# A hybrid decoder layer in float32: another order of the seven products of a block multiplication, with accumulation banks by name

## The chip, the cores and the metric

The kernel runs on one core of one Trainium2 chip. The metric is the device time in microseconds (us); the median of several runs counts. TensorE does the matrix products into PSUM, which has eight banks of 128 x 512 float32; ScalarE (ACT), VectorE (DVE) and GpSimd (POOL) do the element-wise work; nearly all transfers are issued on SyncE's queue (SP).

## The reference, cut to what matters

One layer of a decoder, for 1024 positions and a width of 2048:

```
mod = silu(c) @ W_ada + b_ada              -> shift, scale, gate
h   = rms_norm(x, gain) * (1 + scale) + shift
proj = h @ W_in                            # 2048 x 8192: q k v z (stick-breaking), q k v z (retention)
oa = stick_breaking_attention(norm(q), norm(k), v) * silu(z)    # 8 heads of 128
ob = group_norm(chunkwise_retention(rot(q), rot(k), v)) * silu(z)   # 8 heads of 128
out = x + gate * (concat(oa, ob) @ W_out)  # 2048 x 2048
```

All inputs and the output are float32.

## The kernel before

**Matrix products.** Both large projections are made by a two-by-two block scheme with seven products instead of eight (Winograd's form). The left side is h (or the concatenated heads), transposed, over half of the inner width (1024); its seven block combinations A11, S1, S2, S3, S4, A12, A22 stay in SBUF, each in four pieces of 128 x 512 and each piece as a rounded high part and a low part (`split`: ScalarE makes the high part, L123; VectorE or GpSimd the low part, L124). The right side is a block of 256 columns of the weights, called a *group*. `Group.right` forms what each product needs of it (T1 and T2 on GpSimd), `Group.product` splits it and issues 12 matmuls of 128 x 512 (`mm3`, L127 to L129: four pieces, three matmuls each). The high parts of the weights have four buffers (`wh`), the low parts three (`wl`).

Four results come out of each group, two column halves (i) by two row halves (hf). They are built up in three banks: b takes P1, then P6, then P5, then P3 on top of each other, d takes P7 and then P4, and a takes P2. Between the products the bank is read:

- after P1, ScalarE copies b (`copied`, L272) to p1, and after P2 VectorE adds bank a to it (`added`, L280, or L282 with a gate): result (0,0)
- after P6, ScalarE copies b to u2, and after P4 VectorE adds d: result (0,1)
- after P5, ScalarE copies b to u4 and VectorE adds d: result (1,1)
- after P3, b holds result (1,0), c12

A matmul that adds to a bank, or begins it anew, waits until the bank has been read. The banks are taken in turn from four buffers of one tag, `pj`; the other four banks (A0, A1, B, C) serve the attention work.

**Streams.** `stream` runs a list of groups. P3 and P4 of a group come after P1 of the next one, and after the last group they stand alone. There are five streams: e (16 groups, first half of the inner width, stick-breaking columns; results to `part`), then 32 groups in one stream (f: 16 groups, second half of the inner width, with e's results added to them as a seed, which completes the stick-breaking columns; g: 16 groups, second half, retention columns, results to `part`), then c (16 groups named f too in the profile: first half, whose left side was put by in `keep`, with g's results as a seed, which completes the retention columns; its q and k results are turned by rotary tables in `second_put`, L697 to L703, and written out at L704), then y and o (8 groups each, the two halves of the output projection). The seed is loaded by `old` (L264) and added by GpSimd (L274) behind the copy, or, for c12, by VectorE.

**What sets the order.** TensorE's instructions run in the order in which the program issues them. After each three matmuls of the stream, `run` calls `tick()`, which lets the tasks of two lanes issue their own work (attention heads, preparation of the conditioning, placing of the next left side). The order on the other engines and on SP's queue is chosen by the scheduler of the tile framework, by readiness and priority; products, copies and sums carry a high priority (AHEAD). At the end of a stream, `take` and `gather` replace each left combination as soon as its last product of the stream is issued (`tell`), and the list there gives that order. Tiles of one tag go round over a fixed number of buffers: `pt` (copies, 4 in the streams before the last), `cp` (seeds, 2).

**Retention.** `ret_heads` issues, for each head, the turning of k (`turn_k`), the state updates (`states`), scores (`scores_r`), values (`values_r`) and the normed output's transposes (`finish`), six ticks apart, in banks A0, A1, B and C.

Of the kernel before, what the change touches and what calls it, by code (L numbers as in the profile page):

```python
# [27 lines left out]
RSQRT_MAGIC = 1597463007.0  # L28
AHEAD = 4000
NP = 4  # L30
COMBOS = ("A11", "S3", "S2", "A12", "S1", "S4", "A22")
LEFT = {"P1": "A11", "P7": "S3", "P6": "S2", "P2": "A12", "P5": "S1", "P3": "S4", "P4": "A22"}
SB_GAP = 8
RT_GAP = 6
# [9 lines left out]
def layer_kernel(ctx, tc, x, c, w_ada, b_ada, norm_gain, w_in, sb_q_gain, sb_k_gain, ret_norm_gain, w_out,  # L44
# [158 lines left out]
    class Group:  # L203
# [13 lines left out]
        def right(self, p):  # L217

            t = self.t
            if p == "P1":  # L220
                self.load(0)
                return t["B11"]
            if p == "P7":
                self.load(1)
                t["T1"] = t1 = wp.tile([P, NP, P], F32, tag="wt", bufs=3, name=f"t1_{self.name}")
                nc.gpsimd.tensor_tensor(t1, t["B12"], t["B11"], op=ALU.subtract)
                nc.gpsimd.tensor_tensor(t["B12"], t["B22"], t["B12"], op=ALU.subtract)
                return t["B12"]
            if p == "P6":
                t["T2"] = t2 = wp.tile([P, NP, P], F32, tag="wt", bufs=3, name=f"t2_{self.name}")  # L230
                nc.gpsimd.tensor_tensor(t2, t["B22"], t["T1"], op=ALU.subtract)
                return t2
            if p == "P2":
                return t["B21"]
            if p == "P5":
                return t["T1"]
            if p == "P3":
                return t["B22"]
            nc.gpsimd.tensor_tensor(t["T2"], t["B21"], t["T2"], op=ALU.subtract)
            return t["T2"]  # L240
# [13 lines left out]

    pp = None

    def bank(name):
        return ps.tile([P, HALF], F32, tag="pj", bufs=4, name=name)

    def old(g, i, hf):  # L260

# [2 lines left out]
        nc.sync.dma_start(t, g.seed[i][:, hf * HALF:(hf + 1) * HALF])  # L264
        return t

    def copied(g, src, i, hf, name):

        pool, bufs, _ = g.pool
        t = pool.tile([P, HALF], F32, tag="pt", bufs=bufs, name=f"{name}_{g.name}")  # L270
        gt = g.gate[i]
        nc.scalar.activation(t, src, AF.Copy, scale=1.0 if gt is None else gt)  # L272
# [10 lines left out]

    def stream(groups, after=None):

        prev = None
        tell = after or (lambda n: None)
        for g in list(groups) + [None]:
            if g is not None:
                last = g is groups[-1]  # L290
                if last:
                    tell("")
                g.b = bank(f"b_{g.name}")
                yield from g.product("P1", g.b, True)
                with tc.high_priority(AHEAD):
                    g.p1 = copied(g, g.b, 0, 0, "p1")
                if last:
                    tell("A11")
            if prev is not None:
                q = prev  # L300
                yield from q.product("P3", q.b, False)
                with tc.high_priority(AHEAD):
                    if q.seed is None:
                        c12 = copied(q, q.b, 1, 0, "c12")
                    else:
                        c12 = old(q, 1, 0)
                        added(q, c12, q.b, 1)
                    q.put(1, 0, c12)
                if g is None:
                    tell("S4")  # L310
                yield from q.product("P4", q.d, False)
                with tc.high_priority(AHEAD):
                    added(q, q.u2, q.d, 0)
                    q.put(0, 1, q.u2)
                if g is None:
                    tell("A22")
                if q.done:
                    q.done()
            if g is not None:
                g.d = bank(f"d_{g.name}")  # L320
                yield from g.product("P7", g.d, True)
                if last:
                    tell("S3")
                yield from g.product("P6", g.b, False)
                with tc.high_priority(AHEAD):
                    g.u2 = copied(g, g.b, 0, 1, "u2")
                if last:
                    tell("S2")
                a = bank(f"a_{g.name}")
                yield from g.product("P2", a, True)  # L330
                with tc.high_priority(AHEAD):
                    added(g, g.p1, a, 0)
                    g.put(0, 0, g.p1)
                if last:
                    tell("A12")
# [136 lines left out]
    def first_half(j):  # L472
        for e in range(2):
            for g in range(2):
                to_h(xT[2 * j + e, g], 2 * j + e)
        sums = combine(xT[2 * j, 0], xT[2 * j + 1, 0], xT[2 * j, 1], xT[2 * j + 1, 1],
                       lambda n: st.tile([P, HALF], F32, tag="ht", bufs=7, name=f"{n}_{j}"),
                       nc.vector if j == NP - 1 else nc.gpsimd)
        for n in ("A11", "S3", "S2", "A12", "S1", "A22", "S4"):
            place(n, j, sums[n])  # L480

    x_norms(0)
# [396 lines left out]
    def ret_heads():  # L879
# [5 lines left out]
        for h in range(NH):  # L885
# [33 lines left out]
                                                       up[:, j * P:(j + 1) * P], op0=ALU.mult, op1=ALU.add)  # L919

            def scores_r(g):
                sp = ps.tile([P, 4, P], F32, tag=f"A{g}", name=f"sp_{h}_{g}")
                for j in range(4):
                    tk = slice(j * P, (j + 1) * P)
                    nc.tensor.matmul(sp[:, j, :], k[g][:, tk], q[g][:, tk], start=True, stop=True)
                pTs[g] = pT = ht("T", f"pT{g}")
                nc.vector.tensor_tensor(pT, sp, dm.rearrange("p (a n) -> p a n", a=1).broadcast_to([P, 4, P]),
                                        op=ALU.mult)

            def values_r(g):  # L930
                pT = pTs.pop(g)
                op = ps.tile([P, 4, P], F32, tag=("B", "C")[g], name=f"op_{h}_{g}")
                for j in range(4):
                    cidx = 4 * g + j
                    nc.tensor.matmul(op[:, j, :], pT[:, j, :], v[:, cidx, :], start=True, stop=(cidx == 0))
# [16 lines left out]
                return on, loaded(halves(7 * NH + h, g), f"rz_{h}_{g}")  # L952

            def finish(h, g, on, z):
                tp = ps.tile([P, HALF], F32, tag=("A0", "B")[g], name=f"otp_{h}_{g}")
                for j in range(4):
                    nc.tensor.transpose(tp[:, j * P:(j + 1) * P], on[:, j, :], ident)
                nc.vector.scalar_tensor_tensor(z, tp, ret_g[:, h:h + 1], z, op0=ALU.mult, op1=ALU.mult)
# [53 lines left out]
    start(heads(), 1, 0)  # L1012

    def take(src, needs=()):
        order = ("A11", "S3", "S2", "A12", "S1", "S4", "A22")
        coming = {}

        def tell(n):

            while not needs <= ready:  # L1020
                tick()
            nxt = order[order.index(n) + 1] if n and n != order[-1] else None if n else order[0]
# [104 lines left out]
```

## Time and profile before

| | us |
|---|---|
| median of 3 runs | 2125.51 (2122.24 to 2126.42) |
| profiled execution, its own time | 2124.26 |
| its span, first to last instruction | 2122.3 |
| TensorE busy (matmuls, modelled ends) | 1948.8 (92%) |
| VectorE busy | 1415.7 (67%) |
| ScalarE busy | 965.0 (45%) |
| GpSimd busy | 961.0 (45%) |

A row of waits has the waiting engine, tile and line, then what ended the wait, then the total in us, how often, and the longest. Tile names have their numbers left out: `b_f` is bank b of a group f, `u_f` is u2 or u4, `S_h` the high part of S1 to S4. PE is TensorE, PEld its weight loads. A window's row has the stretch, its length, TensorE's busy time with its instructions, the granted share of its clock, the transfers' share and GB/s.

### The profile page before, as it was taken

To read this page: it belongs to the slowest core of one execution; us is meant where nothing else is said; L and a number is where in the kernel's file an instruction comes from. 1 tells how busy PE (TensorE), PEld (TensorE's weight loads), DVE (VectorE), ACT (ScalarE), POOL (GpSimd) and SP (SyncE) were. 2 spreads that over 40 slices of the span, in tenths; PEclk is the share of its full clock that TensorE was granted. 3 is DMA by queue.
4 is the path that set the end of the run, shared out by engine and by line. 5 is a ranking of instruction groups with operands and counts; after the bars stand their busy time and mean duration, and the time that the engine had idled before them with its cause. 6 is when DMAs were issued, how large, how long until landed. Compare 5 with 4: busy or idle time off the path is not lost. (4 is left out here: it accounts for less than half of the span.)

```text
span 2122.3 us, 28088 instructions
## 1 busy us (share of the span) xinstructions
PE 1948.8 (92%) x9025; PEld 1585.5 (75%) x9025; DVE 1415.7 (67%) x2221; ACT 965.0 (45%) x1771; POOL 961.0 (45%) x850
## 2 busy tenths in 40 slices
PE   5889899898999999999999997898989889998998
PEld 4467777777878777788878885686868767887887
DVE  6677866467768676766564658765776767557554
ACT  5444344354455646455454555453443445335322
POOL 1335575555544544432423244646454453234442
PEclk9879999998999999999999998899999999999999
DMA  9647877423555555563454366656766677556664
GB/s 308 209 159 255 258 256 229 136 86 123 183 156 164 165 164 164 166 192 118 161 160 138 115 206 191 203 168 221 222 221 225 220 235 246 169 173 202 220 208 145
DMA packets 293671, 400.02 MB, mean 188 GB/s; under 512 B 32810, under 2 KB 164980, under 8 KB 293524
## 3 DMA queue, kind: packets, MB, share of 16 engines
q1 hardware_dynamic: 293120, 398.19, 58.6%
q8 instruction: 71, 1.16, 0.2%
q14 instruction: 76, 0.62, 0.1%
q10 hardware_dynamic: 404, 0.05, 0.0%
HBM read 290.05 MB, written 108.10 MB: 188 GB/s over the span
## 5 line engine op out<-in xcount | busy, mean ns | idle before, releaser
L754 DVE TENSOR_TENSOR_SCAN om<-om 128x128 f32<-128x128 f32 (+2 forms) x96 | 107.2, 1117 | 99.6 <-POOL om L744 77.2
L127 PE MATMUL b_f<-S_h,wh_f_P 128*128 128x512 f32 x384 | 157.8, 411 | 15.5 <-ACT u_f L272 15.5
L129 PE MATMUL b_f<-S_h,wl_f_P 128*128 128x512 f32 x384 | 154.3, 402 | 3.9 <-DVE wl_f_P L124 3.9
L128 PE MATMUL b_f<-S_l,wh_f_P 128*128 128x512 f32 x384 | 154.1, 401 | 0.0
L274 POOL TENSOR_TENSOR u_f<-u_f,cp_f 128x512 f32<-128x512 f32 x64 | 88.6, 1385 | 110.5 <-ACT u_f L272 109.5
L124 DVE TENSOR_TENSOR wl_f_P<-wr_f,wh_f_P 128x512 fp32r<-128x512 f32 x128 | 115.6, 904 | 16.6 <-PE b_f L129 4.6
L380 DVE SCALAR_TENSOR_TENSOR acc_b<-ada_b,silu_c,acc_b 128x512 f32<-128x512 f32 x88 | 90.3, 1026 | 37.3 <-DMA ada_b<-in_w_ada_dram 35.7
L123 ACT ACTIVATE wh_f_P<-wr_f 128x512 fp32r<-128x512 f32 x128 | 80.4, 629 | 71.2 <-PE b_f L128 49.1
L127 PEld LDWEIGHTS b_f<-S_h,wh_f_P 128*128 128x128 f32 x384 | 74.6, 194 | 35.8 <-ACT u_f L272 21.2
L127 PE MATMUL b_e<-S_h,wh_e_P 128*128 128x512 f32 x192 | 79.0, 411 | 16.1 <-ACT u_e L272 12.4
L129 PEld LDWEIGHTS b_f<-S_h,wl_f_P 128*128 128x128 f32 x384 | 74.8, 195 | 21.6 <-DVE wl_f_P L124 5.0
L124 DVE TENSOR_TENSOR wl_f_P<-t_f,wh_f_P 128x512 fp32r<-128x512 f32 x96 | 80.7, 841 | 14.1 <-PE b_f L129 11.4
L127 PE MATMUL b_g<-S_h,wh_g_P 128*128 128x512 f32 x192 | 76.2, 397 | 11.2 <-ACT u_g L272 11.1
L128 PEld LDWEIGHTS b_f<-S_l,wh_f_P 128*128 128x128 f32 x384 | 74.7, 195 | 14.6
L123 ACT ACTIVATE wh_f_P<-t_f 128x512 fp32r<-128x512 f32 x96 | 60.2, 628 | 54.9 <-PE a_f L128 16.0
L758 DVE TENSOR_TENSOR be<-be,om 128x128 f32<-128x128 f32 (+2 forms) x96 | 69.5, 724 | 23.3 <-POOL be L746 18.2
L129 PE MATMUL b_e<-S_h,wl_e_P 128*128 128x512 f32 x192 | 78.4, 408 | 5.2 <-DVE wl_e_P L124 5.2
L123 ACT ACTIVATE wh_e_P<-wr_e 128x512 fp32r<-128x512 f32 x64 | 40.2, 628 | 89.9 <-PE b_e L128 65.8
L741 ACT ACTIVATE om<-zp,rq 128x128 f32<-128x128 f32 (+2 forms) x96 | 55.8, 582 | 52.2 <-PE zp L129 36.3
L798 PE MATMUL oT<-a,v 128*128 128x256 f32 x320 | 78.9, 386 | 0.0
L128 PE MATMUL b_e<-S_l,wh_e_P 128*128 128x512 f32 x192 | 77.6, 404 | 0.0
L129 PE MATMUL b_g<-S_h,wl_g_P 128*128 128x512 f32 x192 | 75.7, 394 | 0.1
(388 smaller groups left out, 6407.0 us busy)
## 6 DMA issues: line engine op xcount, KB each, us to landing
ada_b<-in_w_ada_dram SPq DMA_DIRECT2D x128, 256.0 KB
cp_f<-part SPq DMA_DIRECT2D x128, 256.0 KB
wr_f<-in_w_in_dram SPq DMA_DIRECT2D x64, 512.0 KB
wr_e<-in_w_in_dram SPq DMA_DIRECT2D x32, 512.0 KB
ada_a<-in_w_ada_dram SPq DMA_DIRECT2D x64, 256.0 KB
fin<-u_f SPq DMA_DIRECT2D x64, 256.0 KB
wr_g<-in_w_in_dram SPq DMA_DIRECT2D x32, 512.0 KB
vT<-fin SPq DMA_DIRECT2D x48, 256.0 KB
```

The lines of the kernel that those rows point to most:

```text
L123: nc.scalar.activation(hi, src, AF.Copy)
L124: eng.tensor_tensor(lo, src, hi.bitcast(F32), op=ALU.subtract)
L127: nc.tensor.matmul(o, a_hi, b_hi, start=first, stop=False, skip_group_check=True)
L128: nc.tensor.matmul(o, a_hi, b_lo, start=False, stop=False, skip_group_check=True)
L129: nc.tensor.matmul(o, a_lo, b_hi, start=False, stop=last, skip_group_check=True)
L274: nc.gpsimd.tensor_tensor(t, t, old(g, i, hf), op=ALU.add)
L380: nc.vector.scalar_tensor_tensor(acc, src, cj, acc, op0=ALU.mult, op1=ALU.add)
L741: nc.scalar.activation(om[:, :n], zp[:, :n], AF.Sigmoid, scale=rq[:, h, 1, i:i + 1])
L754: nc.vector.tensor_tensor_scan(rev, rev, rev, init, op0=ALU.mult, op1=ALU.bypass)
L758: nc.vector.tensor_tensor(be[:, :n], be[:, :n], om[:, 1:n + 1], op=ALU.mult)
L798: nc.tensor.matmul(ob, v[:, j, :], a[:, cl], start=diag and ib == 0 and b == 0 and j2 == 0, stop=ch == 0 and ib == 2, skip_group_check=True)
```

## The change

The order of the products in the stream is P1, (of the group before: P4, P3), P6, P7, P2, P5 instead of P1, (P3, P4), P7, P6, P2, P5. With it go the lists `COMBOS`, the order of placing in `first_half` and the list in `take`, which become one list `ORDER`.

The fourth result (1,1), u4, is begun by a copy of bank d after P7, and bank b is added to it after P5; before, it was begun by a copy of b after P5, and d was added.

The banks have names: b goes to pj1 and pj0 in turn, and d and a to pj3 and pj2, exchanged from group to group. The turning of x at the start (`turn_x`) takes pj0, A1, pj1, pj2, B, pj3 in turn.

T2 is formed right behind T1, for P6. The copy c12 of groups without a seed takes a `cp` buffer instead of a `pt` buffer.

In retention, `scores_r(0)` takes B instead of A0, `values_r(0)` A0 instead of B, and `finish` of the first half B instead of A0.

```diff
-COMBOS = ("A11", "S3", "S2", "A12", "S1", "S4", "A22")
+ORDER = COMBOS = ("A11", "S2", "S3", "A12", "S1", "A22", "S4")
...
-            if p == "P7":
+            if p == "P6":
                 self.load(1)
                 t["T1"] = t1 = wp.tile([P, NP, P], F32, tag="wt", bufs=3, name=f"t1_{self.name}")
                 nc.gpsimd.tensor_tensor(t1, t["B12"], t["B11"], op=ALU.subtract)
+                t["T2"] = t2 = wp.tile([P, NP, P], F32, tag="wt", bufs=3, name=f"t2_{self.name}")
+                nc.gpsimd.tensor_tensor(t2, t["B22"], t1, op=ALU.subtract)
+                return t2
+            if p == "P7":
                 nc.gpsimd.tensor_tensor(t["B12"], t["B22"], t["B12"], op=ALU.subtract)
                 return t["B12"]
-            if p == "P6":
-                t["T2"] = t2 = wp.tile([P, NP, P], F32, tag="wt", bufs=3, name=f"t2_{self.name}")
-                nc.gpsimd.tensor_tensor(t2, t["B22"], t["T1"], op=ALU.subtract)
-                return t2
...
-    def bank(name):
-        return ps.tile([P, HALF], F32, tag="pj", bufs=4, name=name)
+    def bank(i, name):
+        return ps.tile([P, HALF], F32, tag=f"pj{i}", name=name)
...
-                g.b = bank(f"b_{g.name}")
+                n += 1
+                g.b = bank(n % 2, f"b_{g.name}")
                 yield from g.product("P1", g.b, True)
...
+                yield from q.product("P4", q.d, False)
+                with tc.high_priority(AHEAD):
+                    added(q, q.u2, q.d, 0)
+                    q.put(0, 1, q.u2)
...
                 yield from q.product("P3", q.b, False)
                 with tc.high_priority(AHEAD):
                     if q.seed is None:
-                        c12 = copied(q, q.b, 1, 0, "c12")
+                        c12 = copied(q, q.b, 1, 0, "c12", "cp")
...
-                yield from q.product("P4", q.d, False)
-                with tc.high_priority(AHEAD):
-                    added(q, q.u2, q.d, 0)
-                    q.put(0, 1, q.u2)
...
-                g.d = bank(f"d_{g.name}")
-                yield from g.product("P7", g.d, True)
...
                 yield from g.product("P6", g.b, False)
                 with tc.high_priority(AHEAD):
                     g.u2 = copied(g, g.b, 0, 1, "u2")
...
-                a = bank(f"a_{g.name}")
+                g.d = bank(2 + n % 2, f"d_{g.name}")
+                yield from g.product("P7", g.d, True)
+                with tc.high_priority(AHEAD):
+                    u4 = copied(g, g.d, 1, 1, "u4")
...
+                a = bank(3 - n % 2, f"a_{g.name}")
                 yield from g.product("P2", a, True)
...
                 yield from g.product("P5", g.b, False)
                 with tc.high_priority(AHEAD):
-                    u4 = copied(g, g.b, 1, 1, "u4")
-                    added(g, u4, g.d, 1)
+                    added(g, u4, g.b, 1)
                     g.put(1, 1, u4)
...
-        tag, bufs = (("pj", 4), ("A1", 1), ("pj", 4), ("B", 1), ("pj", 4))[turns % 5]
+        tag, bufs = (("pj0", 1), ("A1", 1), ("pj1", 1), ("pj2", 1), ("B", 1), ("pj3", 1))[turns % 6]
...
-                sp = ps.tile([P, 4, P], F32, tag=f"A{g}", name=f"sp_{h}_{g}")
+                sp = ps.tile([P, 4, P], F32, tag=("B", "A1")[g], name=f"sp_{h}_{g}")
...
-                op = ps.tile([P, 4, P], F32, tag=("B", "C")[g], name=f"op_{h}_{g}")
+                op = ps.tile([P, 4, P], F32, tag=("A0", "C")[g], name=f"op_{h}_{g}")
...
-                tp = ps.tile([P, HALF], F32, tag=("A0", "B")[g], name=f"otp_{h}_{g}")
+                tp = ps.tile([P, HALF], F32, tag="B", name=f"otp_{h}_{g}")
```

More of the change, by code (lines that the diff above doesn't have):

```diff
@@ L265, in old, with copied @@
         return t
-    def copied(g, src, i, hf, name):
-        pool, bufs, _ = g.pool
-        t = pool.tile([P, HALF], F32, tag="pt", bufs=bufs, name=f"{name}_{g.name}")
+    def copied(g, src, i, hf, name, tag="pt"):
+        pool, bufs, old_bufs = g.pool
+        t = pool.tile([P, HALF], F32, tag=tag, bufs=bufs if tag == "pt" else old_bufs, name=f"{name}_{g.name}")
         gt = g.gate[i]
@@ L284, in stream @@
     def stream(groups, after=None):
-        prev = None
+        prev, n = None, 0
         tell = after or (lambda n: None)
@@ L300, in stream @@
                 q = prev
+                yield from q.product("P4", q.d, False)
+                with tc.high_priority(AHEAD):
+                    added(q, q.u2, q.d, 0)
+                    q.put(0, 1, q.u2)
+                if g is None:
+                    tell("A22")
                 yield from q.product("P3", q.b, False)
@@ L310, in stream @@
                     tell("S4")
-                yield from q.product("P4", q.d, False)
-                with tc.high_priority(AHEAD):
-                    added(q, q.u2, q.d, 0)
-                    q.put(0, 1, q.u2)
-                if g is None:
-                    tell("A22")
                 if q.done:
@@ L319, in stream @@
             if g is not None:
-                g.d = bank(f"d_{g.name}")
-                yield from g.product("P7", g.d, True)
-                if last:
-                    tell("S3")
                 yield from g.product("P6", g.b, False)
@@ L328, in stream @@
                     tell("S2")
-                a = bank(f"a_{g.name}")
+                g.d = bank(2 + n % 2, f"d_{g.name}")
+                yield from g.product("P7", g.d, True)
+                with tc.high_priority(AHEAD):
+                    u4 = copied(g, g.d, 1, 1, "u4")
+                if last:
+                    tell("S3")
+                a = bank(3 - n % 2, f"a_{g.name}")
                 yield from g.product("P2", a, True)
@@ L478, in first_half @@
                        nc.vector if j == NP - 1 else nc.gpsimd)
-        for n in ("A11", "S3", "S2", "A12", "S1", "A22", "S4"):
+        for n in ORDER:
             place(n, j, sums[n])
@@ L1014, in take @@
     def take(src, needs=()):
-        order = ("A11", "S3", "S2", "A12", "S1", "S4", "A22")
         coming = {}
@@ L1021, in tell @@
                 tick()
-            nxt = order[order.index(n) + 1] if n and n != order[-1] else None if n else order[0]
+            nxt = ORDER[ORDER.index(n) + 1] if n and n != ORDER[-1] else None if n else ORDER[0]
             if n:
```

## The prediction

> **What bounds the kernel now.** I read the span and clock first, then busy time by stage, then what TensorE waited for, then the timeline around the longest of these waits.
>
> ```profile
> core 0: 2122.3 us, clock 0.966
> 106.80:494.00 387.20, 340.69 (x1442) 0.93 0.60 193
> 494.00:905.00 411.00, 394.09 (x1781) 0.99 0.53 164
> 1297.00:1760.00 463.00, 414.24 (x1992) 0.96 0.67 212
> ```
>
> The windows are the first input stream (e, 16 groups), the first half of the second (f, 16 groups) and the third (c, 16 groups); behind the length stand TensorE's busy time and its clock. TensorE is busy for 340.7 of 387.2, 394.1 of 411.0 and 414.2 of 463.0 us. It bounds every stage, so what the change can win is idle time and half-speed time of TensorE. A group takes 24.2, 25.7 and 28.9 us, so one of its seven products, with the attention work that lies between, takes 3.5, 3.7 and 4.1 us. The bare product is shorter:
>
> ```profile
> 1001.98 0.39 PE L127 MATMUL a_g<-A_h,wh_g_P 128*128 128x512 f32 x1
> 1004.47 0.39 PE L129 MATMUL a_g<-A_h,wl_g_P 128*128 128x512 f32 x1
> ```
>
> These are the first and the last of one product's 12 matmuls: 11 steps in 2.49 us, 0.227 us each, 2.7 us for the product.
>
> Now TensorE's waits (total us, times, longest):
>
> ```profile
> PE b_f L127 <- ACT u_f L272: 15.5, 12, 4.6
> PE b_e L127 <- ACT u_e L272: 12.4, 6, 3.7
> PE b_g L127 <- ACT u_g L272: 11.1, 3, 9.6
> PE sp L925 <- DVE state L918: 10.0, 3, 4.0
> PE d_e L127 <- DVE u_e L280: 9.9, 4, 6.0
> PE b_e L129 <- DVE wl_e_P L124: 8.0, 7, 2.0
> PE b_e L127 <- ACT A_h L123: 6.5, 1, 6.5
> PE a_f L129 <- DVE wl_f_P L124: 5.8, 2, 4.7
> PE b_y L127 <- ACT u_y L272: 4.9, 3, 2.4
> PE b_o L127 <- ACT u_o L272: 4.2, 2, 3.4
> PE b_f L129 <- DVE wl_f_P L124: 3.9, 2, 3.0
> PE b_e L127 <- ACT p_e L272: 3.7, 1, 3.7
> PE d_f L127 <- DVE u_f L280: 2.4, 3, 1.3
> ```
>
> Five rows are waits of the first matmul of P5 or P3 for ScalarE's copy out of bank b (15.5 + 12.4 + 11.1 + 4.9 + 4.2 = 48.1 us, 26 waits). One is P6 waiting for P1's copy (3.7). Two are P4 waiting for VectorE's sum out of bank d (9.9 + 2.4 = 12.3 us, 7 waits). These 64.1 us are what the new order touches. The wl rows are waits for weights, which no order of banks takes away. Five rows of 26 waits over 80 groups also say that the copy is usually in time and only sometimes late.
>
> **The change, part by part.** Every product keeps its 12 matmuls, its split, its copy or sum; nothing is added or removed, so the whole price is in distances.
>
> *P5 and P3 on bank b.* Before, one product lies between P6 and P5 (P2), and one between P5 and P3 (the next group's P1; none in a stream's last group). After, P7 and P2 lie between P6 and P5, P1 and P4 between P5 and P3, and one (P4) in the last group. Each wait shrinks by a product, 2.7 us at least. What stays is what the longest waits have beyond that: 4.6 − 2.7 = 1.9, 3.7 − 2.7 = 1.0, 9.6 − 2.7 = 6.9, 3.4 − 2.7 = 0.7, together 10.5. Gain 48.1 − 10.5 = 37.6 us.
>
> *P4 and P3 against VectorE.* Before, P4 waits for a chain behind P5 (ScalarE copy, GpSimd's addition of the old part where there is one, VectorE's sum), with two products of time. After, the copy of P7 is taken two products before P5 ends, and P3 waits for VectorE's sum alone, also with two products of time. The hop through ScalarE falls away, the lateness of VectorE does not: I take half of 12.3, a gain of 6.1 (bounds 0 and 12.3).
>
> *The first group of a stream.* There is no previous group, so P6 follows P1 directly on one bank; before, P7 lay between. What a direct turn costs at least is shown by the end of the kernel, where P3 follows P5 directly:
>
> ```profile
> 2108.34 0.39 PE L129 MATMUL b_o<-S_h,wl_o_P 128*128 128x512 f32 x1
> 2108.76 0.69 ACT L272 ACTIVATE u_o<-b_o,gate_c 128x512 f32<-128x512 f32 x1 [4.42 <-PE b_o L129]
> 2109.50 0.50 PE L127 MATMUL b_o<-S_h,wh_o_P 128*128 128x512 f32 x1 [0.78 <-ACT u_o L272]
> ```
>
> Four streams lose 0.8 each (3.2), and in the first stream the existing wait of 3.7 grows by the product that hid a part of it, 2.7. Loss 5.9. Banks together: 37.6 + 6.1 − 5.9 = 37.8 us.
>
> *The clock behind a wait.* Windows in which the granted clock was a half:
>
> ```profile
> 323.60:327.00 3.40, 3.14 (x7) 0.50 0.93 327
> 886.80:893.60 6.80, 4.75 (x11) 0.50 0.48 154
> 279.20:282.60 3.40, 3.40 (x9) 0.50 0.72 236
> 1723.00:1726.40 3.40, 3.40 (x10) 0.50 0.92 317
> 1938.10:1941.50 3.40, 3.40 (x10) 0.50 1.04 393
> 1958.50:1962.00 3.50, 3.50 (x9) 0.51 0.01 2
> ```
>
> In the timeline each begins in or just behind one of the waits for a copy. TensorE was busy in them for 3.14 + 4.75 + 3 × 3.40 + 3.50 = 21.6 us, of which half, 10.8, would not be needed at full clock. The one at 886.8 belongs to the 4.6 us wait, of which 1.9 stays; I leave its 2.4 out and take 8.4. The Trainium skill, "TensorE: Matmul & The Clock Gate", Part 1, says that the clock falls to a half after an idle window of about 3.4 us. By it only the first two and the last stretch would count, an estimated (3.14 + 4.75 + 3.50) / 2 = 5.7 us. The trace goes further: the stretch at 1938.1 follows a wait that is at most 2.4 us long, so I stay with the rows.
>
> *What is given back.* A late copy means a late engine, and the same engine makes the weights' two halves:
>
> ```profile
> 887.17 0.63 ACT L687 ACTIVATE sg<-p_f 128x512 f32<-128x512 f32 x1 [4.91 <-issue]
> 887.70 0.61 ACT L123 ACTIVATE wh_g_P<-wr_g 128x512 fp32r<-128x512 f32 x1
> 888.22 0.58 ACT L272 ACTIVATE u_f<-b_f 128x512 f32<-128x512 f32 x1
> ```
>
> Here ScalarE stood for 4.91 us, and the split wh_g waited in the same queue as the copy that held TensorE for 4.6 us. Splits run about two products ahead (their low half has three buffers), so lateness up to two products is absorbed and more is not. I return a third of 37.8 + 8.4 = 46.2, that is 15.4 (bounds 0 and 46.2).
>
> *Buffers of the sums.* For groups with a stored first half, the fourth sum's copy now follows P7 instead of P5, and its buffer is the one the previous group's u2 is written out from. The window between P4 and that copy falls from four products to three. In the third stream the q and k groups (8 of 16) turn their sums by the rotary tables before the write:
>
> ```profile
> 1576.87 0.39 PE L129 MATMUL d_f<-A_h,wl_f_P 128*128 128x512 f32 x1
> 1589.32 0.32 SPq L704 DMA_DIRECT2D fin<-u_f  x1
> 875.50 0.46 SPq L599 DMA_DIRECT2D rawq<-fin  x1
> 879.03 0.63 ACT L123 ACTIVATE q<-rawq 128x512 fp32r<-128x512 f32 x1 [4.85 <-DMA rawq<-fin]
> ```
>
> P4 ended at 1577.3 and the write was issued at 1589.3, 12.1 us later; a transfer of the same 256 KB took 3.5 us from issue to use, so the buffer is free after 15.6 us. Three products are 3 × 4.1 = 12.4: ScalarE may wait 3.2 us, in eight groups 25.6. Behind it in ScalarE's queue stand the splits; their lead of two products (8.2 us) covers most, so I take 5 (bounds 0 and 25.6). The load of the old part on SP's queue likewise waits for c12's write; it has two products instead of five before GpSimd asks for it, and VectorE's sum stands two products behind.
>
> *Retention, end, start.* scores_r(0) moves from A0, freed by the state operations (the 10.0 us row), to B, freed by the late head's gate product, which is behind them on VectorE in seven heads of eight:
>
> ```profile
> L958 DVE SCALAR_TENSOR_TENSOR rz<-otp,cols,rz x16: 733/743/752, 1516.6 to 1873.7; 128x512 f32<-128x512 f32 x16
> 2116.13 1.09 PE L1064 MATMUL ytp<-ident,u_o 128*128 128x128 f32 x8
> ```
>
> It could lose 7 × 0.74 = 5.2 us or, where that product runs earlier, win the 10.0; I take 0. At the end the last product is now P3, whose sum the first eight output transposes read; before, these ran while P4's sum was made. Eight took 1.1 us in the row: loss 0.9. The turning of x I cost at nothing: the same matmuls and copies go over six banks before and after, only the order in which the banks come round is another.
>
> **Sum.** 46.2 − 15.4 − 5 − 0.9 = 24.9 us less than the profiled execution's 2124.3 us (span 2122.3 and 2.0 around it), 2099.4; the median is 1.2 above that execution, so 2101.
>
> **The rivals.**
> *Slower: the new copy blocks ScalarE.* One mechanism: in the eight rotary groups of the third stream u4's copy waits for u2's write (3.2 us) and then the old part's load for c12's write (3.5 us), and ScalarE and VectorE pass it on to the splits. At full price that is 8 × 6.7 = 53.6 in place of the 5, so 2101 + 48.6 = 2150; it makes the kernel slower from (24.9 + 5) / 8 = 3.7 us per group on; at 5 us it gives 2136. For it: the 12.1 us row, and waits for wl in this very stream up to 4.7. Against it: 3.2 is under the 8.2 of lead. The Trainium skill, "Perfetto Trace Analysis", Tensor Engine Instruction, calls ScalarE, VectorE and GpSimd strict FIFO; the 4.91 us row agrees.
> *No change.* All lateness returns as waits for weights: 2124 to 2127, if not a third but nine tenths of the 46.2 come back. For it: the 4.91 us row; against it: most waits are under 2.7 us.
> *More.* Nothing returned, no buffer wait: 46.2 − 0.9 = 45.3, so 2080.
>
> **How the numbers follow.** A difference of 0.2% (4.3 us) is about what a measurement of this kernel can tell. Forecast 0.58, more 0.10, no change 0.13, slower 0.19. Some 0.02 of the no-change case lie beyond 4.3 us on the fast side: faster 0.58 + 0.10 + 0.02 = 0.70, same 0.11, slower 0.19. The forecast's own range, with a fifth to a half returned and 0 to 15 for the buffers, is 2086 to 2112. The full range reaches from the larger gain, 2080, to 2132, which leaves out the upper part of the slower case (some 0.12) and little below.
>
> **What would show it.** Right: the rows of b_f, b_e, b_g, b_y, b_o waiting for L272 shrink from 48 us to about 12; P6 of each stream's first group waits for the copy p; rows of wl grow by some 10 us; stretches at half clock between 270 and 330 and near 887, 1723, 1938 vanish. Wrong: ScalarE idle before the copy u in the third stream, ended by a DMA of fin, with wl rows there above 20 us; or sp still waiting, for L958. If the b rows vanish and the span stays, the splits took it all.

## The result, and the profile after

The changed kernel is a little slower: median 2129.71 us of 18 runs against 2123.70 us of 18 runs of the kernel before, ratio 1.003 with a 95% interval of 1.0017 to 1.0044. The prediction had 2101 us, with 2086 to 2112 as its forecast's own range.

Span and clock after:

```profile
core 0: 2126.1 us, clock 0.967
```

The seven stretches after (start, e, f, g, c, y, o: each from the first matmul of a stream to the next one's; length, TensorE's busy time, its clock):

```profile
0.00:108.80 108.80, 72.46 (x386) 0.95 0.77 252
108.80:491.50 382.70, 338.89 (x1442) 0.93 0.60 193
491.50:900.00 408.50, 382.34 (x1699) 0.97 0.51 160
900.00:1308.60 408.60, 399.01 (x1850) 0.99 0.49 156
1308.60:1769.70 461.10, 413.76 (x1992) 0.96 0.67 215
1769.70:1948.50 178.80, 175.72 (x866) 1.00 0.61 199
1948.50:2126.10 177.60, 168.87 (x801) 0.99 0.62 197
```

The same stretches before, where they differ most (f, g, y):

```profile
493.90:880.20 386.30, 374.01 (x1699) 1.00 0.53 166
880.20:1297.30 417.10, 399.65 (x1850) 0.98 0.49 157
1760.10:1943.80 183.70, 178.15 (x866) 0.99 0.60 199
```

The loss sits in one stage. f, the groups that complete the stick-breaking columns while attention runs, grew from 386.3 to 408.5 us; g gave back 8.5, y 4.9, e 4.4, c 1.7 and o 0.9, and the start took 2.0 more. In f both parts grew: TensorE's idle time from 12.3 to 26.2 us (length less busy time), and its busy time by 8.3 at a clock that fell from 1.00 to 0.97. These lengths are of one profiled execution each; f is 405.6 to 407.0 us in three more runs of the changed order with the seeds on SP's queue (a later fourth seed, retention's old banks, a buffer of its own for c12), and 387.3 in the old order with the fourth sum begun from d.

TensorE's waits after. First those at the banks of the products, then those for weights, then attention's:

```profile
PE b_e L127 <- ACT p_e L272: 7.6, 2, 6.5
PE b_e L127 <- DVE u_e L280: 6.6, 1, 6.6
PE b_g L127 <- DVE u_g L280: 5.1, 2, 3.2
PE b_f L127 <- ACT p_f L272: 4.2, 2, 3.2
PE b_o L127 <- ACT p_o L272: 3.1, 1, 3.1
PE b_f L127 <- DVE u_f L280: 1.8, 2, 1.4
PE b_y L127 <- DVE u_y L282: 1.2, 1, 1.2
PE b_y L127 <- ACT p_y L272: 1.1, 1, 1.1
...
PE d_f L129 <- DVE wl_f_P L124: 10.1, 6, 3.8
PE b_f L129 <- DVE wl_f_P L124: 7.9, 6, 2.4
PE b_e L129 <- DVE wl_e_P L124: 7.5, 5, 3.6
PE d_e L129 <- DVE wl_e_P L124: 5.1, 6, 2.0
PE a_e L129 <- DVE wl_e_P L124: 3.8, 3, 1.5
PE a_f L129 <- DVE wl_f_P L124: 3.4, 4, 1.8
...
PE ms L659 <- ACT be L744: 10.1, 5, 4.1
PE vtp_vT L639 <- DVE z L803: 8.3, 2, 6.3
PE zp L127 <- ACT sq L661: 7.7, 3, 3.9
PE sp L927 <- DVE rz L960: 7.1, 3, 3.8
```

Attention's three rows before:

```profile
PE ms L657 <- ACT be L742: 4.5, 4, 2.6
PE vtp_vT L637 <- DVE z L801: 4.5, 1, 4.5
PE zp L127 <- ACT sq L659: 4.0, 3, 1.8
```

At the banks 30.7 us are left of 64.1. The six rows for weights have 37.8 us; with the smaller ones all waits for weights are 40.4, where they were 19.9. All waits of attention's matmuls (ms, vtp, zp, sp, op, up, otp) are 47.6 where they were 37.6: ms, vtp and the row of zp rose from 13.0 to 26.1, sp fell from 10.0 to 7.1 and op from 7.3 to 4.5. So of the 33.4 us that left the banks 30.5 came back at other matmuls.

In f itself little was to be won at the banks: 3.7 us of waits there became 1.0. All waits of ms and all in the row of zp shown lie in f. Together with 2.0 of vtp, attention's waits in f rose from 8.5 to 19.8 us, and those for weights from nothing to 5.3.

Why f: the seeds are the first suspect. Each group there loads four seeds into two buffers. Some of SP's waits at the seed loads (L264) over the whole kernel, before in the first fence and after in the second, and GpSimd's wait for a seed to land:

```profile
SPq L264 <- DMA fin<-cp_f: 24.9, 17, 3.7
```

```profile
SPq L264 <- DMA fin<-cp_f: 47.9, 20, 5.4
SPq L264 <- DMA cp_f<-part: 23.8, 13, 3.8
POOL u_f L274 <- DMA cp_f<-part: 20.2, 10, 3.5
```

The wait for c12 to be written out doubled, and the other two rows are new. In f alone the first is smaller, 7.7 us before and 15.2 after. All of SP's waits at L264 in f rose from 112 to 174 us, and 104 and 142 of them were ended by GpSimd, which has to add a seed before its buffer is free. How that can reach TensorE is seen in one place of the timeline after (start, length, what):

```profile
586.70 4.69 SPq L264 DMA_DIRECT2D cp_f<-part  x3
589.74 1.30 POOL L274 TENSOR_TENSOR u_f<-u_f,cp_f 128x512 f32<-128x512 f32 x1 [3.08 <-DMA cp_f<-part]
591.97 0.37 SPq L601 DMA_DIRECT2D rawq<-fin  x1
595.91 0.63 ACT L123 ACTIVATE q<-rawq 128x512 fp32r<-128x512 f32 x1 [2.45 <-DMA rawq<-fin]
597.62 0.79 PE L659 MATMUL ms<-shi,mean_r 128*128 128x512 f32 x1 [4.11 <-ACT be L744]
```

SP issues three seed loads over 4.69 us, the last only after GpSimd has added an earlier one; the load of q behind them goes out at 591.97; ScalarE stands 2.45 us for it until 595.91, its two sigmoids of scores (the second is `be`, L744) come after that, and ms waits 4.11 us for bank A0, which they read.

### The profile page after: what moved, and what is told of

Its sections match the earlier page's. It is cut to its first block, busy times and chain, and to the rows that moved or that the text cites. A ratio compares the mean times of both kernels' runs of the same rounds, so it can differ in the third digit from the quotient of the medians.

```text
span 2126.1 us, 28003 instructions
## 1 busy us (share of the span) xinstructions
PE 1951.0 (92%) x9025; PEld 1586.9 (75%) x9025; DVE 1432.3 (67%) x2221; ACT 963.8 (45%) x1771; POOL 958.0 (45%) x850
## 5 line engine op out<-in xcount | busy, mean ns | idle before, releaser
L382 DVE SCALAR_TENSOR_TENSOR acc_b<-ada_b,silu_c,acc_b 128x512 f32<-128x512 f32 x88 | 96.7, 1099 | 34.3 <-DMA ada_b<-in_w_ada_dram 33.0
L124 DVE TENSOR_TENSOR wl_f_P<-wr_f,wh_f_P 128x512 fp32r<-128x512 f32 x128 | 109.8, 858 | 5.7 <-issue 4.4
L123 ACT ACTIVATE wh_f_P<-wr_f 128x512 fp32r<-128x512 f32 x128 | 80.6, 630 | 66.0 <-PE b_f L128 23.6
L231 POOL TENSOR_TENSOR wr_f<-wr_f,wr_f 128x512 f32<-128x512 f32 x32 | 48.7, 1521 | 108.4 <-DMA wr_f<-in_w_in_dram 100.2
L127 PE MATMUL b_e<-S_h,wh_e_P 128*128 128x512 f32 x192 | 78.6, 409 | 14.7 <-ACT p_e L272 7.6
L124 DVE TENSOR_TENSOR wl_f_P<-t_f,wh_f_P 128x512 fp32r<-128x512 f32 x96 | 86.2, 898 | 6.8 <-PE b_f L129 5.0
L123 ACT ACTIVATE wh_f_P<-t_f 128x512 fp32r<-128x512 f32 x96 | 60.3, 628 | 54.2 <-PE b_f L128 27.4
L239 POOL TENSOR_TENSOR t_f<-wr_f,t_f 128x512 f32<-128x512 f32 x32 | 45.8, 1432 | 78.5 <-DVE wl_f_P L124 40.5
L760 DVE TENSOR_TENSOR be<-be,om 128x128 f32<-128x128 f32 (+2 forms) x96 | 66.3, 691 | 19.9 <-POOL be L748 15.5
```

The lines of the kernel that those rows point to most:

```text
L123: nc.scalar.activation(hi, src, AF.Copy)
L124: eng.tensor_tensor(lo, src, hi.bitcast(F32), op=ALU.subtract)
L127: nc.tensor.matmul(o, a_hi, b_hi, start=first, stop=False, skip_group_check=True)
L382: nc.vector.scalar_tensor_tensor(acc, src, cj, acc, op0=ALU.mult, op1=ALU.add)
L760: nc.vector.tensor_tensor(be[:, :n], be[:, :n], om[:, 1:n + 1], op=ALU.mult)
```

## The experiments

The lines of each edit are cut to what matters. All ratios are to the kernel before. The expectations count f as 419 us in the changed order, some ten more than the 408.5 measured here from f's first matmul to g's first, so their figures for f are best read as differences.

**Three seed buffers, in both orders.** The room comes from retention's state, split over a free operand buffer and a smaller tile. The same split is in the runs without loads, with four buffers for the low halves and with a buffer of its own for c12, in both orders; it was not run alone, so what it does by itself is not known.

```diff
-            self.pool = pool or (pp, 4, 2)
+            self.pool = pool or (pp, 4, 3)
```

> The changed kernel with three buffers instead of two for the seeds (cp); the room comes from retention's state, which is split over a free operand buffer and a smaller tile. Queue theory: in the f groups SP's queue stands at the seed loads (L264) because a seed buffer is still being read or written out, 110 us in total before and 170 after in the stretch 491 to 906; behind it the loads of q and k and the writes of the mean squares come late, and ScalarE and VectorE, in order, pass it on to ms and zp in bank A0. With a third buffer these waits fall under 110 us, the f stage falls from 419 to 402 to 408 us and the ratio to the kernel before is 0.993 to 0.998. Split theory: the lateness comes back through the weights' splits whatever the queue does; the wl rows stay near 41 us and the ratio stays at 1.003.

> The kernel before with the same third seed buffer. Queue theory: there the seed of u4 is asked for five products behind the write that frees its buffer, so the third buffer is worth little: ratio 0.997 to 1.000, less than in the changed kernel. Split theory: 1.000.

Measured: changed order 2119.53 us, 0.9978 (0.9963 to 0.9992); old order 2122.35 us, 0.9989 (0.9977 to 1.0001). The third buffer, with the split, is worth 0.5% to the changed order and 0.1% to the old one, as the queue theory had it. Its interval in the old order includes no change. But the f stage came down to 401.7 us only, not to the old order's length, which with three buffers is 385.7:

```profile
488.70:890.40 401.70, 378.26 (x1700) 0.98 0.52 163
```

and SP's wait for c12's write stayed (49.4 us). The row of SP waiting for a seed to land is gone.

**The fourth sum's beginning, taken alone both ways.** The changed order with u4 begun from b again, and the old order with u4 begun from d.

```diff
# changed order
-                    u4 = copied(g, g.d, 1, 1, "u4")        # after P7
...
-                    added(g, u4, g.b, 1)                   # after P5
+                    u4 = copied(g, g.b, 1, 1, "u4")
+                    added(g, u4, g.d, 1)
```

> The changed kernel with the fourth sum begun from bank b after P5 again and d added. Queue theory: u4's seed is asked for two products later, so the f stage comes back to about 404 us, but P4 now has only P1 between itself and VectorE's sum out of d, where the kernel before has P1 and P3: rows of d waiting for L280 rise from 0 to 15 to 30 us; ratio 1.000 to 1.006. Split theory: no gain in f, only the loss at d: ratio 1.006 to 1.012.

> The kernel before with only the fourth sum begun from d after P7 and b added after P5, in the old order of products. Queue theory: u4's seed is asked for two products earlier, so the f stage loses 8 to 15 us; P3 has only P1 between itself and VectorE's sum out of b, where it had ScalarE's copy: ratio 1.004 to 1.012. Split theory: only the second of these, ratio 1.000 to 1.006.

Measured: 2197.91 us, 1.0349 (1.0323 to 1.0376), and 2136.29 us, 1.0049 (1.0033 to 1.0066). In the new order with the old beginning, P4 meets VectorE's sum far more than expected (first fence); in the old order with the new beginning, P3 does (second fence):

```profile
PE d_f L127 <- DVE u_f L280: 64.2, 23, 7.9
PE d_e L127 <- DVE u_e L280: 39.4, 9, 13.7
```

```profile
PE b_f L127 <- DVE u_f L280: 27.6, 12, 5.3
PE b_e L127 <- DVE u_e L280: 25.0, 6, 12.0
```

So order and beginning belong together: each alone loses more than both. The expected loss of 8 to 15 us in f for the second run did not come (387.3 us against 386.3), nor did f shrink in the first (406.6). Its seeds fall otherwise than I had counted: u4's takes over the buffer of p1's, and u2's that of c12, three products behind it.

**No seeds, and no loads of seeds.** Four kernels, two in each order. In the first pair the seeds are neither loaded nor added; in the second the loads alone are left out and a tile of zeros is added.

```diff
# first pair
-        if g.seed is not None:
-            nc.gpsimd.tensor_tensor(t, t, old(g, i, hf), op=ALU.add)
# second pair
-        nc.sync.dma_start(t, g.seed[i][:, hf * HALF:(hf + 1) * HALF])
...
-            nc.gpsimd.tensor_tensor(t, t, old(g, i, hf), op=ALU.add)
+            nc.gpsimd.tensor_tensor(t, t, flat_seed(), op=ALU.add)
```

> The changed kernel with the seeds left out: the stored first halves are neither loaded nor added, and c12 is a copy by ScalarE everywhere, so the output lacks them. Queue theory (seed loads on SP and seed additions on GpSimd make the f stage late): with them gone the changed order keeps its gain at the banks; its f stage is not longer than that of the old order without seeds, and its time is 15 to 30 us under that kernel's. Lateness theory (ScalarE and VectorE are late by themselves, and TensorE meets them at the next place where it needs them): f stays 8 us or more longer than in the old order without seeds, and the two times are within 8 us.

> The kernel before with the seeds left out in the same way; the reference for the run above. Both theories: some 20 to 40 us under the kernel before, as GpSimd and SP have less to do.

> The changed kernel with the loads of the seeds left out and their additions kept: GpSimd and VectorE add a tile of zeros, so the output lacks the first halves. Queue theory (the loads on SP and the seed buffers they wait for): the changed order gains over the old order as much as without seeds altogether, 10 to 20 us, and the f stage is no longer than in the old order. Additions theory (GpSimd's three and VectorE's one addition per group come at worse times in the new order): the changed order is within 5 us of the old one, and f is 8 us or more longer.

> The kernel before with the loads of the seeds left out in the same way; the reference for the run above. Both theories: between the kernel without seeds (2070) and the kernel before (2124), nearer to the former by the queue theory, nearer to the latter by the additions theory.

Measured: without seeds 2053.93 us, 0.9668 (0.9654 to 0.9682) in the changed order and 2070.47 us, 0.9746 (0.9730 to 0.9762) in the old. Without loads 2100.00 us, 0.9890 (0.9867 to 0.9912), and 2111.54 us, 0.9949 (0.9931 to 0.9966). Changed order over old order is 1.0030 with seeds, 0.9890 / 0.9949 = 0.9941 without loads and 0.9668 / 0.9746 = 0.9920 without seeds. Of the swing of 1.1% (23 us) between the first and the last, the loads carry 0.9% (19 us, with some 7 either way by the intervals). The 0.2% (4 us) left for the additions is within the intervals. With three seed buffers the changed order is at 0.9978 / 0.9989 = 0.9989 of the old one, so the third buffer alone takes about 9 of the 19 us. The f stage in the second pair, changed and old:

```profile
489.10:881.40 392.30, 376.61 (x1700) 0.99 0.40 125
```

```profile
496.50:882.30 385.80, 373.58 (x1699) 1.00 0.40 126
```

22.2 us of difference have become 6.5: most of f's loss goes when the loads go. In f attention's waits at ms, zp and vtp, 19.8 us against 8.5 with loads, are 11.0 against 6.8 without them. The expectation that f would be no longer was too strong; without seeds f is 376.0 us against 372.3. Two more expectations missed: the old order without seeds is 53 us under the kernel before, not 20 to 40, and without loads it is nearer to the kernel before (12 us under it) than to the kernel without seeds (41 us over it), which had been named as a sign of the additions theory. In the old order the additions thus seem to cost more than the loads; it is the difference between the orders that goes with the loads. The transfers as such are not short of room: with the loads f's DMA share was 0.51 in the changed order and 0.53 in the old.

**The fourth seed one product later.**

```diff
-                    u4 = copied(g, g.d, 1, 1, "u4")
+                    u4 = copied(g, g.d, 1, 1, "u4", seeded=False)
...
                     g.put(0, 0, g.p1)
+                    seed(g, u4, 1, 1)                      # after P2
```

> The changed kernel with the seed of the fourth sum loaded and added one product later: the copy of d is still taken after P7, the seed is asked for after P2. Queue theory: SP's waits at L264 in the f stage fall from 170 towards 110 us, f falls from 419 to about 405 us, ratio 0.993 to 0.998. Lateness theory: f within 5 us of 415, ratio 0.999 to 1.004.

Measured: 2131.82 us, 1.0033 (1.0021 to 1.0045). SP's waits at L264 in f did not fall (172 us) and f is 407.0 us, as the lateness theory had it. Asking one product later for u4's seed makes no difference.

**Four buffers for the weights' low halves.**

```diff
-                lo = wp.tile([P, NP, P], F32R, tag="wl", bufs=3, ...)
+                lo = wp.tile([P, NP, P], F32R, tag="wl", bufs=4, ...)
```

> The changed kernel with four buffers instead of three for the low halves of the weights (room as in the run with three seed buffers), so that the splits may run three products ahead. Split theory: of the 39 us of waits for weights half or more go, ratio 0.992 to 0.997. Queue theory and lateness theory: VectorE makes the low halves when it gets to them, the waits stay over 28 us; ratio 1.000 to 1.004.

Measured: 2142.34 us, 1.0096 (1.0079 to 1.0113). The weights' waits fell, from 40.4 to 15.4 us, as the split theory had it, and the time rose. The rows of banks took over:

```profile
PE b_e L127 <- DVE u_e L280: 18.6, 5, 11.5
PE b_f L127 <- DVE u_f L280: 8.8, 5, 2.8
PE b_e L129 <- DVE wl_e_P L124: 4.6, 2, 2.3
```

VectorE's sums for e and f, 6.6 and 1.8 us with three buffers, have 18.6 and 8.8. Before the longest of these waits (11.5 us, until 495.2) VectorE works without a stop from 479.2 us on, for the most part at low halves of the next left side; two splits of weights among them take 2.9 us. So a weights' split that stands before a sum is a part of that wait at most.

The f stage, though, nearly came back:

```profile
500.50:893.20 392.70, 376.55 (x1700) 0.98 0.52 166
```

That is 15.8 us less than the changed kernel's 408.5 and as short as without the loads (392.3), with all seeds loaded; SP's waits at L264 in f fell from 174 to 114 us. So f's loss is not the loads' alone: it goes as well when the splits have more room. The kernel is slower because other stages lost more, e 9 us and c 19 (480.2 against 461.1).

**Retention's banks as they were.**

```diff
-                sp = ps.tile([P, 4, P], F32, tag=("B", "A1")[g], ...)
+                sp = ps.tile([P, 4, P], F32, tag=f"A{g}", ...)
```

> The changed kernel with retention's banks as they were (scores in A0 and A1, values in B and C, the transposes in A0 and B). By the prediction the new dealing costs 0 to 5 us: ratio 1.000 to 1.003, sp waiting for L918 again. If the new dealing is a gain: 1.004 to 1.008.

Measured: 2132.48 us, 1.0046 (1.0028 to 1.0064), which overlaps the 1.0017 to 1.0044 of the changed kernel. The row of sp came back as expected:

```profile
PE sp L927 <- DVE state L920: 11.8, 4, 5.2
```

With the new dealing sp waits 7.1 us for VectorE's gate product (L960), without it 11.8 for the state. The medians differ by 2.8 us in favour of the new dealing; these runs do not tell that from nothing.

**P7 ahead of P6 in a stream's first group, with three seed buffers.**

```diff
+                if prev is not None:
+                    yield from six()                       # P6 and its copy
                 g.d = bank(2 + n % 2, f"d_{g.name}")
                 yield from g.product("P7", g.d, True)
...
+                if prev is None:
+                    yield from six()
```

> The changed kernel with three seed buffers and, in the first group of each stream alone, P7 ahead of P6, so that a product lies between P1 and P6 there. The five waits for the copy p after a direct turn (6.5, 3.2, 3.1, 1.1 and 1.0 us) shrink by up to 2.7 each, 8 us together if nothing takes their place: ratio 0.994 to 0.996 where three buffers alone had 0.998. If ScalarE and VectorE are the ones that are late, half of it comes back: 0.996 to 0.998.

Measured: 2117.68 us, 0.9981 (0.9969 to 0.9994), the same as three buffers alone and just outside both expectations. The waits for p shrank to 5.4 us, of which this row is the larger part:

```profile
PE b_e L127 <- ACT p_e L273: 4.8, 2, 3.7
```

With three buffers alone they were 22.0 us (8.9, 6.5, 4.5 and 2.1 for e, f, y and o), in the changed kernel 16.0. So 16.6 us of waits went, and the time did not follow.

**The seed loads on another queue.**

```diff
-        nc.sync.dma_start(t, g.seed[i][:, hf * HALF:(hf + 1) * HALF])
+        nc.gpsimd.dma_start(t, g.seed[i][:, hf * HALF:(hf + 1) * HALF])    # or nc.scalar
```

> The changed kernel with the seed loads issued on GpSimd's queue instead of SP's; buffers and additions as they are. If SP standing at the seed loads is what costs (everything behind it on SP is late): the loads of q and k and the writes of the mean squares no longer wait, the f stage falls from 419 to about 405 us, ratio 0.992 to 0.997, unless issuing costs GpSimd more than 0.3 us each. If the seeds' own lateness is what costs (GpSimd's addition waits for the load): f stays at 415 or more, ratio 1.001 or above.

> The kernel before with its seed loads on GpSimd's queue, the reference for the price of issuing there. SP standing: ratio 0.997 to 1.000, a smaller gain than in the changed kernel. Seeds' own lateness: 1.000 to 1.005.

> The changed kernel with the seed loads issued on ScalarE's queue. SP is free of them as in the run on GpSimd's queue, but ScalarE now stands until a seed buffer is free, and the copies and the high halves stand behind it. If a stand on SP costs, one on ScalarE costs more: ratio 1.005 to 1.03, with waits of TensorE for L272 and L123. If the buffers are usually free by then: 0.993 to 1.000.

> The changed kernel with three seed buffers and the seed loads on GpSimd's queue. If SP standing and the buffers' release are two costs: better than either alone, ratio 0.989 to 0.994, near the 0.989 without loads. If they are one cost: as the better of the two alone, 0.995 to 0.998.

Measured: GpSimd's queue 2146.11 us, 1.0106 (1.0088 to 1.0124), in the changed order; 2122.80 us, 0.9993 (0.9978 to 1.0008), in the old; 2138.78 us, 1.0067 (1.0049 to 1.0084), in the changed order with three buffers. ScalarE's queue 2168.40 us, 1.0204 (1.0183 to 1.0224). Freeing SP of the loads did not help the changed order as a whole; both other places are worse, and with three buffers neither expectation was met. On GpSimd's queue f became a little shorter (403.5 us), while c grew from 461.1 to 478.0. On ScalarE's queue the ratio is as expected, but TensorE pays at attention's bank and not at L272 and L123:

```profile
PE ms L659 <- ACT be L744: 16.7, 7, 4.7
PE zp L127 <- ACT sq L661: 16.2, 7, 6.1
```

On GpSimd's queue 160 loads also take GpSimd's own time:

```profile
0.00:2145.10 2145.10, 88.91 (x160) 0.97 0.58 186
```

That is 0.56 us for each, above the 0.3 us that the expectation had set as its condition. The old order bears the same 160 loads without loss, the changed order loses 16 us by them. So this does not clear SP; it suggests that the changed order has no slack on GpSimd either. The Trainium skill, "Trainium Kernel Development and Optimization", Key Constraints, says that issuing from several engines only saves issue time, as all queues feed the same transfer engines; the old order agrees (0.9993), the changed order does not: there the place of issue is worth 0.8% (1.0106 against 1.0030) and on ScalarE's queue 1.7% (1.0204). That loads which wait for their buffer hold up the work behind them on that engine would fit the rows of ms and zp above, but no run here separates this from the price of issuing.

**A buffer of its own for c12, in both orders.**

```diff
-        t = pool.tile([P, HALF], F32, tag="cp", bufs=bufs, ...)
+        tag, bufs = ("cs", 1 if bufs == 2 else 2) if (i, hf) == (1, 0) else ("cp", 2 if bufs == 2 else 3)
+        t = pool.tile([P, HALF], F32, tag=tag, bufs=bufs, ...)
```

> The changed kernel with a buffer of its own for c12 (cs) and the two seed buffers left to the other three seeds; as much room as with three seed buffers in turn. If it is c12's long hold (until it is written out) that the next seeds meet, the row of L264 waiting for the write of c12 (47.9 us) goes, and the ratio is 0.991 to 0.996, better than the 0.998 of three buffers in turn. If the hold is not what counts but the number of buffers: 0.997 to 0.999. If neither: 1.002 to 1.004.

> The kernel before with a buffer of its own for c12, the reference: there the seed that takes over c12's buffer is asked for five products later, so 0.997 to 1.000 by all three.

Measured: 2123.80 us, 0.9998 (0.9985 to 1.0012), in the changed order, 2121.32 us, 0.9984 (0.9970 to 0.9998), in the old. The changed order wins 0.3%, perhaps less than by three buffers in turn, whose interval (0.9963 to 0.9992) overlaps. None of the three expectations fits: it lies between the second and the third. Nor did the edit take c12's hold away: SP's row of waits for its write is still 47.0 us in 20 waits, as now c12's next seed meets it. So whether the hold counts is not shown, only that more buffers help a little; f is 405.6 us.

## Why the prediction was wrong, point by point

*P5 and P3 on bank b:* right, and more than forecast. 10.5 of the 48.1 us were to stay; no row of a b bank waiting for ScalarE's copy u is left.

*P4 and P3 against VectorE:* wrong. 12.3 us were to fall by half; TensorE now waits 14.7 us for VectorE's sums (6.6, 5.1, 1.8 and 1.2), at P3 instead of P4.

*The first group of a stream:* the mechanism was right, the term too small. A loss of 5.9 us was worked out from the smallest direct turn, 0.8; the rows for p_e, p_f, p_o and p_y are 16.0 us (1.1 of them inside stream e) against 3.7 before, a loss of 12.3. The growth in the first stream, to 6.5 us, is as forecast; the other streams lose more than 0.8. At the start of o, for one, ScalarE makes high halves of the new left side until just before p's copy, and TensorE waits 3.1 us. But winning these waits back, with three seed buffers, did not shorten the kernel.

Banks together were to lose 37.8 us and lost 33.4. That the sum is so near is luck: the first part gained 10.5 more than forecast, the second and the third 8.5 and 6.4 less.

*The clock behind a wait:* wrong. 8.4 us were to come; the mean clock went from 0.966 to 0.967, and in f, where the idle time more than doubled, it fell from 1.00 to 0.97.

*What is given back:* the step that failed first. I returned a third, 15.4 us, and only as waits for weights. These rose by 20.5 us, and attention's waits, which I had not put in, by 10.0. Together that is 30.5 against the 33.4 that left the banks: nine tenths were given back. The prediction let ScalarE make both halves of the weights; VectorE makes the low halves, and it is for these that TensorE now waits. The run with a fourth buffer for the low halves shows the exchange from the other side, weights' waits turned into banks' waits. That exchange alone would have made the no-change rival true.

*Buffers of the sums:* the step that failed in size and place. I costed the tighter buffers at 5 us, at ScalarE's copy in the third stream, and mentioned the seeds' load on SP's queue in a sentence without a price. The pairs without loads and with them put the price of the seeds' loads at about 19 us of difference between the orders, a third buffer takes about 9 of them, and the f stage lost 22.2 us, 6.5 without loads. The third stream, where I had placed it, did not lose (462.8 to 461.1), and ScalarE has no wait there before a copy u.

*Retention, end, start:* retention was taken at 0, and is not told from 0. The sign named against it did come: sp still waits for the gate product, 7.1 us, where it had waited 10.0 for the state.

*Readings:* the window given for f, 494 to 905, reaches 25 us into g; f is 386.3 us, a group of it 24.1 and a product with its attention work 3.4, not 25.7 and 3.7. The sum does not use these. The forecast's own range does not follow from its terms: with a fifth to a half returned and 0 to 15 for the buffers they give about 2090 to 2118, not 2086 to 2112. The measured 2129.71 lies outside both.

*The rivals:* the result, ratio 1.003, is what the slower rival's sign says, but not its mechanism: no stand of ScalarE at u4's copy in the rotary groups. It is the no-change rival's return of lateness plus a cost in another stage that goes, for the larger part, with the seed loads.

What is shown: that without the seeds' loads the changed order is about 12 us faster than the old one and with them 6 us slower, that a third seed buffer, together with the split of retention's state, brings the changed order below the old kernel, and that banks, weights and attention exchange waits. What is argued from single places of the trace: the path from SP's stand over the load of q to ms. What stays open: why f still lost 6.5 us without the loads; which of the seeds' releases counts, since neither a later fourth seed nor a buffer of its own for c12 nor another queue settled it; how the splits and the seeds hang together in f, where a fourth buffer for the low halves did as much as leaving the loads out; and what T2's earlier forming, c12's copy in a `cp` buffer and the other turns of x did, which no run takes apart.

The version that beats both kernels is the changed order with three seed buffers, 0.9978 (0.9963 to 0.9992). Much of that is not the new order's doing: the old order with the same room has 0.9989, and with a buffer of its own for c12 0.9984, whose intervals overlap with it.

## What to carry to other kernels

A wait that disappears from the bounding engine is won only if the engine that was late catches up; where TensorE runs in program order and another engine is two thirds busy, as VectorE is here, sum the waits over all kinds of matmuls, not over those that the edit touches. When an order of steps is changed, list for each ring of buffers the distance between each release and the next request, the loads' queue included: here the loads into a ring of two buffers made a difference of about 19 us between two orders, half of which a third buffer took away, though no single request could be named as the cause. A part of a change tried alone can lose (1.035 and 1.005) where the whole is nearly even, so parts are judged together.

## What the runs showed that I had not expected

Leaving out 160 loads of 256 KB made the changed kernel 1.4% faster (1.0030 to 0.9890) and the old one 0.5% (0.9949). One more weights' buffer, with the split of retention's state, made the kernel 0.7% slower (1.0096 against 1.0030), though it shortened f by 15.8 us. A load issued by GpSimd took it 88.91 / 160 = 0.56 us.
